# One pool for the feed-forward part, down's operand halves in freed slots, and early sum chains in a seven-product SwiGLU

## The chip, the core and the metric

The kernel runs on one core of a Trainium2 chip. The metric is the device time of one execution in microseconds (us). TensorE (PE in the profile) multiplies; ScalarE (ACT) and VectorE (DVE) convert, add and copy; GpSimd (POOL) and SyncE (SP) here mostly start DMAs. A DMA that adds to what is in the tile (an accumulating DMA) is started by POOL, a plain load by SP. Each engine works through a list of instructions whose order was fixed when the kernel was built; an instruction that waits holds up all behind it on its engine.

## The reference, cut to what matters

Two layers: a dilated-window attention layer and a gated-linear-attention layer (GLA), each followed by a feed-forward part. With 512 tokens, width 1024 and hidden width 2816, that part is

```python
def swiglu(h, w_gate_up, w_down):
    g, u = jnp.split(h @ w_gate_up, 2, axis=-1)
    return (jax.nn.silu(g) * u) @ w_down
# h += swiglu(rms_norm(h, ffn_norm[i]), ffn_w_gate_up[i], ffn_w_down[i])
```

It is run twice: FFN0 after attention, FFN1 after GLA. All is float32. To reach that accuracy each operand is split into a high part (rounded to the type fp32r) and a low part (what is left), and each product is three matmuls: high·high, high·low, low·high.

## The kernel before, in words

**A split** (`split`, lines 88 to 94) is one ACT instruction that writes the high tile (L92) and one DVE instruction that writes the low tile (L93). Weights arrive by DMA in a raw tile (`wf`, two buffers, or `wA`, `wB`) and are split into `wh` and `wl` (three buffers each).

**Order.** The Tile framework fixes each engine's order at build time. It takes instructions as they become ready in its own model, the ones with the smaller program number first; `high_priority(offset=AHEAD)` lowers the numbers by 100. A tile has a tag, and a tag a number of buffers; a new tile waits until one of its tag's buffers has been released by all its users. Pools are opened and closed per stage; a tile in a new pool waits for the tiles of the closed pool whose memory it overlaps (`reuse_waits="tile"`).

**Gate and up by seven products.** `gate_up` (L302) runs over six chunks, j = 0 to 5, of hidden columns: five of 512, the last of 256. Each chunk has gate and up columns, and tokens and input features are halved, so that a chunk is a 2x2 by 2x2 block product; it is computed with seven products instead of eight. The weight blocks 0 to 3 are combined as they are loaded. For each chunk `forms` (L221) is a generator that yields the weights of the seven products in the order in which they are used:

| product | left side | weights | where the raw weights come from |
|---|---|---|---|
| first | A11 | block 0 | `wA`, loaded by SP |
| second | A12 | block 1 | `wf`, loaded by SP |
| fifth | S1 | 0+2 | block 2 added onto `wA` by a POOL DMA, after the first product's split has read `wA` |
| sixth | S2 | 0+2+3 | DVE adds block 3 (`wB`) to `wA` |
| third | S4 | 3 | `wB`; block 1 is then added onto `wA` by a POOL DMA |
| seventh | S3 | 3+2 | block 2 added onto `wB` by a POOL DMA, after the third product's split has read `wB` |
| fourth | A22 | 0+2+3+1 | `wA` |

A chunk of 512 has two tiles of each (n = 2), the last chunk one (n = 1). The last chunk already loads blocks 0 and 3 twice, so that it need not wait for a split before it adds; all of these loads and adds stand in `first()`. `wA` has four buffers and `wB` two, so that a later chunk's loads start when an earlier chunk's buffers come free. A product of a 512-wide chunk is 24 matmuls (`product`, L287). S1 to S4 are sums of the normed input's blocks, made by `block_sums` (L184) on ACT and DVE and split into `sh` and `sl`; the splits of A11 to A22 are made while the stage before writes its last results. While a chunk is multiplied, the four results of the chunk before are transposed on PE and copied by ACT (`turn`, L319): 22 tiles `acts`, the first 8 in tag `h`, the other 14 in tag `a`.

**Pools.** `swiglu` (L212) opens an outer pool with the `a` tiles, in it a pool `GATE_UP` (`sh`, `sl`, `wA`, `wB`, `g`, `Rc`), closes that and opens a pool `DOWN` with 40 half-size tiles `ah`.

**Down.** The 22 `acts` are split and multiplied with down's weights, eight output blocks m of 22 x 3 matmuls. The splits of acts 0 and 1 go to free `xs` tiles during the last chunk, and their six matmuls run before the last eight transposes; the splits of acts 2 to 21 follow in `down` (L408), in `ah` tiles.

Of the kernel before, what the change touches and what calls it, by code (L numbers as in the profile page):

```python
# [12 lines left out]
F32 = mybir.dt.float32  # L13
# [7 lines left out]
P = 128  # L21
# [16 lines left out]
class Trunk:  # L38
    def __init__(self, ctx, tc, ins):
# [10 lines left out]
    ATTN = {"qk": 20, "v": 8, "zs": 4, "wa": 4, "wb": 2, "sm": 3, "pt": 2, "ob": 2, "on": 2, "ao": 4,  # L50
            "tab": 2, "masks": 1, "ms": 1, "Rc": 1, "ebias": 1, "mst": 1,
            "qv": 2, "qr": 2, "qtmp": 2, "st": 2, "t2": 2, "stn": 2, "st0": 2, "mw": 2, "mL": 5}
    FFN = {"a": NH - KT}
    GATE_UP = {"sh": 4, "sl": 4, "wA": 4, "wB": 2, "g": 7, "Rc": 8}
    DOWN = {"ah": 2 * NH - 4}
    GLA = {"qk": 8, "r": 8, "v": 8, "wg": 1, "z": 1, "rs": 2, "A": 2, "qs": 6, "kT": 6, "e": 4, "y": 1, "c": 1, "wa": 3,
           "state": 6, "later": 1, "reset": 1, "Rc": 1, "mid": 2, "full": 4}
    PBUFS = {"pp": 4, "s": 2, "t": 1, "o": 1}
# [153 lines left out]
    def swiglu(self, layer, col_next):  # L212
        with self.phase(f"ffn{layer}", self.FFN):
            acts = []
            outer = self.local
            with self.phase(f"gate_up{layer}", self.GATE_UP):
                self.gate_up(layer, acts, outer)
            with self.phase(f"down{layer}", self.DOWN):
                self.down(layer, acts, col_next)

    def forms(self, dram, ahead=0):  # L221
        nc = self.nc
        n = dram.shape[1]
        raw = {}

        def load(block, tag):
            raw[tag] = []
            for i in range(n):
                w = self.t(tag, (P, 1024))
                nc.sync.dma_start(w, dram[block, i])  # L230
                raw[tag].append(w)

        def add(tag, block):
            for i in range(n):
                nc.gpsimd.dma_start(raw[tag][i], dram[block, i], accum_op=ALU.add)

        def ready(tag):
            return [self.split(w, (P, 1024), "wh", "wl") for w in raw[tag]]

        def first():  # L240
            load(0, "wA")
            if n == 1:
                whole = raw["wA"]
                load(0, "wA")
                add("wA", 2)
                load(3, "wB")
                raw["wC"] = raw["wB"]
                load(3, "wB")
                add("wB", 2)
                return [self.split(w, (P, 1024), "wh", "wl") for w in whole]  # L250
            return ready("wA")

        def second():
            load(1, "wf")
            return ready("wf")

        def fifth():
            if n > 1:
                add("wA", 2)
                load(3, "wB")  # L260
                raw["wC"] = raw["wB"]
            return ready("wA")

        def sixth():
            for i in range(n):
                nc.vector.tensor_add(raw["wA"][i], raw["wA"][i], raw["wC"][i])
            return ready("wA")

        def third():
            add("wA", 1)  # L270
            return ready("wC")

        def seventh():
            if n > 1:
                add("wB", 2)
            return ready("wB")

        def fourth():
            return ready("wA")

        for step in (first, second, fifth, sixth, third, seventh, fourth):
            with self.tc.high_priority(offset=AHEAD + ahead):
                w = step()
            ahead = 0
            yield w
# [13 lines left out]
                mm(a, lhsT=xh[:, tok], rhs=wl[:, f], start=False, stop=False, skip_group_check=True)  # L299
                mm(a, lhsT=xl[:, tok], rhs=wh[:, f], start=False, stop=k == last, skip_group_check=True)  # L300

    def gate_up(self, layer, acts, outer):  # L302
        nc = self.nc
        self.col0 = 16 + 8 * layer
        ACT, DVE = nc.scalar.activation, nc.vector
        weights = [self.forms(self.ins["gate_up"][layer, j], 0 if j else 2 * AHEAD) for j in range(5)]
        weights.append(self.forms(self.ins["gate_up_last"][layer]))
        first = next(weights[0])
        self.minus = self.t("Rc", (P, 8))
        DVE.tensor_scalar(self.minus[:, 0:4], self.cols[:, self.col0 + 4:self.col0 + 8], -1.0, None, op0=ALU.mult)  # L310
        sums = [self.block_sums(m) for m in range(KT // 2)]
        self.kept = self.dr.tile([KT, P, S], F32, name=f"h_dram_{layer}")
        cut = lambda lo: [tuple(e[:, lo:lo + 256] for e in self.x[m]) for m in range(KT // 2, KT)]
        A11, A12, A22 = self.x[0:KT // 2], cut(0), cut(256)
        S3, S1, S2, S4 = ([s[i] for s in sums] for i in range(4))

        done = None

        def turn(c):  # L319
            if done is None:  # L320
                return
            pt = self.p("to"[c % 2])
            for i in range(NT):
                nc.tensor.transpose(pt[:, i * P:(i + 1) * P], done[i // 2][:, i % 2, c * P:(c + 1) * P], self.ident)
            if len(acts) < KT:
                a = self.t("h")
            else:
                self.n += 1
                a = outer.tile([P, S], F32, tag="a", name=f"a_{self.n}", bufs=NH - KT)
            ACT(a, pt, AF.Copy)  # L330
            acts.append(a)

        for j in range(6):
            width = 512 if j < 5 else 256
            w = weights[j]
            pair = lambda tag: [self.p(tag) for _ in range(2)]
            keep = lambda: self.t("g", (P, 2, S))

            def copy(src):
                out = keep()  # L340
                for i in range(2):
                    ACT(out[:, i, 0:width], src[i][:, 0:width], AF.Copy)
                return out

            b1 = pair("pp")
            self.product(b1, A11, first if j == 0 else next(w), width, True)
            turn(0)
            g1 = copy(b1)
            b2 = pair("pp")
            self.product(b2, A12, next(w), width, True)  # L350
            turn(1)
            if j == 0:
                for m in range(KT):
                    self.add_square(m, self.h[m], ("sq", "R")[m % 2])
                R = self.token_norm()
                for m in range(KT):
                    nc.gpsimd.dma_start(self.kept[m], self.h[m])
            for i in range(2):
                e = g1[:, i, 0:width]
                DVE.tensor_add(e, b2[i][:, 0:width], e)  # L360
                silu = ACT(e, e, AF.Silu, scale=R[:, i:i + 1])
            b3 = pair("s")
            self.product(b3, S1, next(w), width, True)
            turn(2)
            p5 = copy(b3)
            self.product(b1, S2, next(w), width, False)
            turn(3)
            h1 = copy(b1)
            self.product(b3, S4, next(w), width, False)
            for i in range(2):  # L370
                e = h1[:, i, 0:width]
                DVE.tensor_add(e, b3[i][:, 0:width], e)
                DVE.scalar_tensor_tensor(e, e, R[:, 4 + i:5 + i], g1[:, i, 0:width], op0=ALU.mult, op1=ALU.mult)
            self.product(b1, S3, next(w), width, False)
            h2 = copy(b1)
            for i in range(2):
                e = h2[:, i, 0:width]
                DVE.tensor_add(e, p5[:, i, 0:width], e)
            self.product(b1, A22, next(w), width, False)
            g2 = keep()  # L380
            for i in range(2):
                e = g2[:, i, 0:width]
                silu = ACT(e, b1[i][:, 0:width], AF.Silu, scale=R[:, 2 + i:3 + i])
                u = h2[:, i, 0:width]
                DVE.scalar_tensor_tensor(u, u, R[:, 6 + i:7 + i], e, op0=ALU.mult, op1=ALU.mult)
            done = (h1, h2)
            if j == 4:
                with self.tc.high_priority(offset=AHEAD):
                    early = [self.split(a, (P, S), "xs", "xs") for a in acts[0:2]]
        self.started = self.down_part(self.p("pp"), layer, 0, 0, 2, early)  # L390
        for c in range(2):
            turn(c)
        with self.tc.issue_after(silu.ins):
            nc.scalar.preload_act_table_set("natural_log_exp_and_others")

    def down_part(self, ps, layer, m, k, end, pairs):
        for k0, kn in ((0, 8), (8, 8), (16, 6)):
# [10 lines left out]
    def down(self, layer, acts, col_next):  # L408
        nc = self.nc
        ps, pairs = self.started  # L410
        for k in range(2, NH):
            if k < 8:
                with self.tc.high_priority(offset=AHEAD):
                    pairs.append(self.split(acts[k], (P, S), "ah", "ah"))
            else:
                pairs.append(self.split(acts[k], (P, S), "ah", "ah"))
        self.x = [None] * KT
        for m in range(KT):
            if m > 0:
# [656 lines left out]
```

## Time and profile before

| what | value |
|---|---|
| median of 3 runs | 1584.66 us (1582.45 to 1586.26) |
| the profiled execution | 1582.96 us |
| its span, first to last instruction | 1581.2 us |
| ACT, busy share of the span | 49% |
| DVE, busy share of the span | 60% |
| mean TensorE clock granted | 0.992 |
| moved by DMA | 179.74 MB |

The profile describes one execution. PE is nearly always busy, so what matters are the few places where it waits: a row such as `[3.71 <-ACT wh L92]` says that PE sat idle for 3.71 us before the instruction and that ACT's write of a `wh` tile in line 92 ended the wait. The granted clock (PEclk) is a share of full speed.

FFN0 multiplies from about 632 us of the span, its down part from 864 us; FFN1 from about 1224 us, its down part from 1454 us.

### The profile page before, as it was taken

The numbers are of one execution on the slowest core, as the hardware profiler recorded it, in microseconds if no ns is written. First come the engines' busy times: TensorE is split into PE (matmuls) and PEld (weight loads), VectorE is DVE, ScalarE is ACT, GpSimd is POOL, SyncE is SP. The second block draws the span as 40 slices with busy tenths as digits, with TensorE's granted clock in tenths as the row PEclk, the third lists the DMA queues.
The fourth block names the chain that finished last, engine by engine and source line by source line (L and its number), as shares of the span: only waits on it lengthen the run. The fifth ranks groups of instructions, "written<-read, shape, count | busy, mean of one in ns | idle before, by whom it ended". The sixth has DMA issues, their size and how long they took to land.

```text
span 1581.2 us, 21054 instructions
## 1 busy us (share of the span) xinstructions
PE 1550.1 (98%) x8078; PEld 1257.4 (80%) x8078; DVE 949.4 (60%) x1714; ACT 780.0 (49%) x1319; POOL 104.1 (7%) x180
## 2 busy tenths in 40 slices
PE   8999999999999999999999999999999999999999
PEld 7878787887877877788888888777778788878887
DVE  6574656666467656866666533756566766657421
ACT  6343443445345554665556422544564665556311
POOL 0001010101000001111110000000001111110000
PEclk9999999999999999999999999999999999999999
DMA  8422222242221215567674432311126567664331
GB/s 281 137 68 93 70 81 80 68 132 81 88 65 50 71 36 194 132 148 173 160 160 104 117 102 78 108 67 67 60 74 212 147 160 169 155 145 107 120 119 65
DMA packets 58964, 179.74 MB, mean 114 GB/s; under 512 B 9936, under 2 KB 10512, under 8 KB 58864
## 3 DMA queue, kind: packets, MB, share of 16 engines
q1 hardware_dynamic: 45776, 135.27, 26.1%
q0 software_dynamic: 13088, 43.13, 14.3%
q8 instruction: 63, 1.03, 0.3%
q14 instruction: 37, 0.30, 0.1%
HBM read 169.91 MB, written 8.46 MB: 113 GB/s over the span
## 4 chain that ended last, share of the span: by engine, by line
PE 75%; issue 13%; DVE 5%; ACT 3%; DMA 2%; POOL 2%; POOLq 0%; SPq 0%; ACTq 0%; DVEq 0%
PE ppp L511 8%; PE ppp L509 8%; PE ppp L510 8%; PE ppp L105 8%; PE ppp L104 8%; PE ppp L106 8%; PE po L618 4%; PE ppp L298 3%; PE ppp L299 3%; PE ppp L300 3%; DMA wB<-in_gate_up_dram 2%; PE ps L686 2%; PE pt L556 1%; PE ps L636 1%; PE po L938 1%
## 5 line engine op out<-in xcount | busy, mean ns | idle before, releaser
L93 DVE TENSOR_TENSOR wl<-wf,wh 128x1024 fp32r<-128x1024 f32 (+1 forms) x180 | 213.5, 1186 | 208.6 <-ACT wh L92 207.6
L92 ACT ACTIVATE wh<-wf 128x1024 fp32r<-128x1024 f32 (+1 forms) x180 | 185.5, 1031 | 303.4 <-PE ppp L105 179.1
L509 PE MATMUL ppp<-wh,xs 128*128 128x512 f32 (+1 forms) x672 | 263.4, 394 | 5.4 <-ACT wh L92 5.4
L511 PE MATMUL ppp<-wh,xs 128*128 128x512 f32 (+1 forms) x672 | 263.1, 392 | 0.0
L510 PE MATMUL ppp<-wl,xs 128*128 128x512 f32 (+1 forms) x672 | 262.6, 391 | 0.0
L509 PEld LDWEIGHTS ppp<-wh,xs 128*128 128x128 f32 x672 | 128.2, 191 | 30.6 <-ACT wh L92 5.4
L511 PEld LDWEIGHTS ppp<-wh,xs 128*128 128x128 f32 x672 | 128.1, 191 | 23.4
L510 PEld LDWEIGHTS ppp<-wl,xs 128*128 128x128 f32 x672 | 128.4, 191 | 22.5 <-DVE wl L93 1.2
L93 DVE TENSOR_TENSOR wl<-wA,wh 128x1024 fp32r<-128x1024 f32 x88 | 107.2, 1221 | 48.3 <-ACT wh L92 48.3
L104 PE MATMUL ppp<-ah,wh 128*128 128x512 f32 x320 | 125.6, 392 | 2.2 <-ACT ah L92 2.2
L105 PE MATMUL ppp<-ah,wh 128*128 128x512 f32 x320 | 125.7, 393 | 0.5 <-DVE ah L93 0.5
L106 PE MATMUL ppp<-ah,wl 128*128 128x512 f32 x320 | 125.0, 391 | 0.0
L92 ACT ACTIVATE wh<-wA 128x1024 fp32r<-128x1024 f32 x88 | 92.5, 1056 | 51.1 <-PE ppp L300 37.6
L298 PE MATMUL ppp<-wh,xs 128*128 128x512 f32 (+1 forms) x288 | 108.4, 384 | 4.6 <-ACT wh L92 3.7
L299 PE MATMUL ppp<-wl,xs 128*128 128x512 f32 (+1 forms) x288 | 107.9, 375 | 1.3 <-DVE wl L93 1.3
L300 PE MATMUL ppp<-wh,xs 128*128 128x512 f32 (+1 forms) x288 | 107.7, 374 | 0.0
L93 DVE TENSOR_TENSOR wl<-wB,wh 128x1024 fp32r<-128x1024 f32 x44 | 53.9, 1224 | 86.7 <-ACT wh L92 86.7
L105 PE MATMUL ppp<-xs,wh 128*128 128x512 f32 x256 | 103.7, 405 | 1.1 <-DVE xs L93 1.1
L104 PE MATMUL ppp<-xs,wh 128*128 128x512 f32 x256 | 103.4, 405 | 0.0
L106 PE MATMUL ppp<-xs,wl 128*128 128x512 f32 x256 | 102.9, 402 | 0.0
L583 ACT ACTIVATE sm<-sm,st 128x160 f32<-128x160 f32 (+2 forms) x128 | 56.9, 446 | 43.0 <-DVE st L582 41.5
L299 PE MATMUL ppp<-wl,sh 128*128 128x512 f32 (+1 forms) x192 | 73.0, 380 | 4.7 <-DVE wl L93 4.7
(281 smaller groups left out, 2933.2 us busy)
## 6 DMA issues: line engine op xcount, KB each, us to landing
wA<-in_gate_up_dram POOLq DMA_DIRECT2D x40, 512.0 KB, 5.4
wf<-in_down_dram SPq DMA_DIRECT2D x32, 512.0 KB, 3.6
wf<-in_a_w_v_dram SPq DMA_DIRECT2D x20, 512.0 KB, 3.6
wf<-in_gate_up_dram SPq DMA_DIRECT2D x20, 512.0 KB, 5.0
wA<-in_gate_up_dram SPq DMA_DIRECT2D x20, 512.0 KB, 4.3
wB<-in_gate_up_dram SPq DMA_DIRECT2D x20, 512.0 KB, 3.3
wB<-in_gate_up_dram POOLq DMA_DIRECT2D x20, 512.0 KB, 5.8
wf<-in_a_w_q_dram SPq DMA_DIRECT2D x16, 512.0 KB, 3.2
```

Source lines behind the costliest of these rows:

```text
L92: nc.scalar.activation(hi, src, AF.Copy)
L93: nc.vector.tensor_sub(lo, src, hi.bitcast(F32))
L104: mm(out, lhsT=wh, rhs=xh, start=start, stop=False)
L105: mm(out, lhsT=wh, rhs=xl, start=False, stop=False)
L106: mm(out, lhsT=wl, rhs=xh, start=False, stop=stop)
L298: mm(a, lhsT=xh[:, tok], rhs=wh[:, f], start=start and k == 0, stop=False, skip_group_check=True)
L299: mm(a, lhsT=xh[:, tok], rhs=wl[:, f], start=False, stop=False, skip_group_check=True)
L300: mm(a, lhsT=xl[:, tok], rhs=wh[:, f], start=False, stop=k == last, skip_group_check=True)
L509: mm(a, lhsT=xh, rhs=wh[:, f], start=k == 0, stop=False)
L510: mm(a, lhsT=xh, rhs=wl[:, f], start=False, stop=False)
L511: mm(a, lhsT=xl, rhs=wh[:, f], start=False, stop=k == KT - 1)
L618: self.nc.tensor.matmul(o, lhsT=pts[b][c], rhs=vals(i0 + b, c), start=c == 0, stop=c == 1)
```

## The change

1. `swiglu` opens one pool for gate, up and down together. The pool `DOWN` and its `ah` tiles go away.
2. `halves(a, k)` replaces the splits of acts 2 to 21: the high and the low part stand in one (128, 1024) tile, in a buffer of the tags that gate and up have finished with: `wA` for k = 2 to 5, `wB` for 6 and 7, `sh` for 8 to 11, `sl` for 12 to 15, `g` for 16 to 21.
3. The halves of acts 2 to 7 are traced at the end of `gate_up`, ahead of down's first six matmuls and of the last transposes, with high priority. Before, they were traced in `down`.
4. In chunk 0 and in the last chunk (`own`), `first()` loads block 0 into `wf`. Their sums get raw tiles of their own, which no split reads first: `sums()` loads block 0 into `wA` and adds block 2, loads block 3 into `wB` and once more into a second `wA` buffer, and adds block 2 onto that. `sums()` stands at the head of `second()`, ahead of the load of block 1. Chunk 0 so loads blocks 0 and 3 twice, as the last chunk did before: four more loads of 512 KB in each feed-forward part. Chunks 1 to 4 are as before.

```diff
-    FFN = {"a": NH - KT}
-    GATE_UP = {"sh": 4, "sl": 4, "wA": 4, "wB": 2, "g": 7, "Rc": 8}
-    DOWN = {"ah": 2 * NH - 4}
+    FFN = {"a": NH - KT, "sh": 4, "sl": 4, "wA": 4, "wB": 2, "g": 7, "Rc": 8}
...
         with self.phase(f"ffn{layer}", self.FFN):
             acts = []
-            outer = self.local
-            with self.phase(f"gate_up{layer}", self.GATE_UP):
-                self.gate_up(layer, acts, outer)
-            with self.phase(f"down{layer}", self.DOWN):
-                self.down(layer, acts, col_next)
+            self.gate_up(layer, acts)
+            self.down(layer, acts, col_next)
...
+        def sums():
+            load(0, "wA")
+            add("wA", 2)
+            load(3, "wB")
+            raw["wC"] = raw["wB"]
+            load(3, "wB", "wA")
+            add("wB", 2)
+
         def first():
-            load(0, "wA")
-            if n == 1:
-                whole = raw["wA"]
+            if not own:
                 load(0, "wA")
-                add("wA", 2)
-                load(3, "wB")
-                raw["wC"] = raw["wB"]
-                load(3, "wB")
-                add("wB", 2)
-                return [self.split(w, (P, 1024), "wh", "wl") for w in whole]
-            return ready("wA")
+                return ready("wA")
+            load(0, "wf")
+            return ready("wf")
 
         def second():
+            if own:
+                sums()
             load(1, "wf")
             return ready("wf")
...
-        weights = [self.forms(self.ins["gate_up"][layer, j], 0 if j else 2 * AHEAD) for j in range(5)]
-        weights.append(self.forms(self.ins["gate_up_last"][layer]))
+        weights = [self.forms(self.ins["gate_up"][layer, j], j == 0, 0 if j else 2 * AHEAD) for j in range(5)]
+        weights.append(self.forms(self.ins["gate_up_last"][layer], True))
...
+        with self.tc.high_priority(offset=AHEAD):
+            early += [self.halves(acts[k], k) for k in range(2, 8)]
         self.started = self.down_part(self.p("pp"), layer, 0, 0, 2, early)
...
+    def halves(self, a, k):
+        nc = self.nc
+        tag = "g" if k > 15 else "sl" if k > 11 else "sh" if k > 7 else "wB" if k > 5 else "wA"
+        both = self.t(tag, (P, 1024), F32R)
+        hi, lo = both[:, 0:S], both[:, S:]
+        nc.scalar.activation(hi, a, AF.Copy)
+        nc.vector.tensor_sub(lo, a, hi.bitcast(F32))
+        return hi, lo
...
-        for k in range(2, NH):
-            if k < 8:
-                with self.tc.high_priority(offset=AHEAD):
-                    pairs.append(self.split(acts[k], (P, S), "ah", "ah"))
-            else:
-                pairs.append(self.split(acts[k], (P, S), "ah", "ah"))
+        for k in range(len(pairs), NH):
+            pairs.append(self.halves(acts[k], k))
```

In the parts that the diff cuts, `fifth()` and `seventh()` test `own` where they tested n, and a tile of `turn` is taken from the one pool.

More of the change, by code (lines that the diff above doesn't have):

```diff
@@ L214, in swiglu, with forms @@
             acts = []
-            outer = self.local
-            with self.phase(f"gate_up{layer}", self.GATE_UP):
-                self.gate_up(layer, acts, outer)
-            with self.phase(f"down{layer}", self.DOWN):
-                self.down(layer, acts, col_next)
-    def forms(self, dram, ahead=0):
+            self.gate_up(layer, acts)
+            self.down(layer, acts, col_next)
+    def forms(self, dram, own, ahead=0):
         nc = self.nc
@@ L224, in forms, with load @@
         raw = {}
-        def load(block, tag):
+        def load(block, tag, at=None):
             raw[tag] = []
             for i in range(n):
-                w = self.t(tag, (P, 1024))
+                w = self.t(at or tag, (P, 1024))
                 nc.sync.dma_start(w, dram[block, i])
@@ L257, in fifth @@
         def fifth():
-            if n > 1:
+            if not own:
                 add("wA", 2)
@@ L273, in seventh @@
         def seventh():
-            if n > 1:
+            if not own:
                 add("wB", 2)
@@ L300, in product, with gate_up @@
                 mm(a, lhsT=xl[:, tok], rhs=wh[:, f], start=False, stop=k == last, skip_group_check=True)
-    def gate_up(self, layer, acts, outer):
+    def gate_up(self, layer, acts):
         nc = self.nc
@@ L324, in turn @@
                 nc.tensor.transpose(pt[:, i * P:(i + 1) * P], done[i // 2][:, i % 2, c * P:(c + 1) * P], self.ident)
-            if len(acts) < KT:
-                a = self.t("h")
-            else:
-                self.n += 1
-                a = outer.tile([P, S], F32, tag="a", name=f"a_{self.n}", bufs=NH - KT)
+            a = self.t("h" if len(acts) < KT else "a")
             ACT(a, pt, AF.Copy)
@@ L410, in down @@
         ps, pairs = self.started
-        for k in range(2, NH):
-            if k < 8:
-                with self.tc.high_priority(offset=AHEAD):
-                    pairs.append(self.split(acts[k], (P, S), "ah", "ah"))
-            else:
-                pairs.append(self.split(acts[k], (P, S), "ah", "ah"))
+        for k in range(len(pairs), NH):
+            pairs.append(self.halves(acts[k], k))
         self.x = [None] * KT
```

## The prediction

> **What bounds the kernel now.** I read the page first, then the waits of PE by stage, then the stretches around them.
>
> ```profile
> PE 1550.1 (98%) x8078; PEld 1257.4 (80%) x8078; DVE 949.4 (60%) x1714; ACT 780.0 (49%) x1319; POOL 104.1 (7%) x180
> ```
>
> ```profile
> 799.41 0.39 PE L300 MATMUL ppp<-wh,xs 128*128 128x512 f32 x1
> ...
> 804.85 0.40 PE L300 MATMUL ppp<-wh,xs 128*128 128x512 f32 x1
> ```
>
> PE is the bound. In steady state 24 matmuls take 804.85 - 799.41 = 5.44 us: 0.227 each, 5.44 a product. The change removes no matmul, so it can win only what PE loses around the feed-forward parts. The rows of PE's waits there, as total, times and longest:
>
> FFN0, start (627 to 638 us):
>
> ```profile
> PE ppp L298 <- ACT wh L92: 3.7, 1, 3.7
> PE ppp L299 <- DVE wl L93: 1.3, 1, 1.3
> ```
>
> FFN0, end of chunk 0 (663 to 674):
>
> ```profile
> PE ppp L299 <- DVE wl L93: 1.5, 2, 0.8
> PE ppp L298 <- ACT g L342: 0.9, 1, 0.9
> PE ppp L298 <- ACT wh L92: 0.2, 1, 0.2
> ```
>
> FFN1, end of chunk 0 (1251 to 1260):
>
> ```profile
> PE ppp L299 <- DVE wl L93: 1.0, 2, 0.8
> PE ppp L298 <- ACT wh L92: 0.3, 1, 0.3
> ```
>
> Chunk 4 in FFN0 (827 to 834), then in FFN1 (1397 to 1420):
>
> ```profile
> PE ppp L299 <- DVE wl L93: 1.2, 2, 0.7
> ```
>
> ```profile
> PE ppp L299 <- DVE wl L93: 1.0, 2, 0.8
> PE ppp L298 <- ACT wh L92: 0.8, 1, 0.8
> ```
>
> Start of down, FFN0 and FFN1, from PE's timeline:
>
> ```profile
> 866.61 0.33 PE L324 MATMUL pt<-ident,g 128*128 128x128 f32 x1 [0.52 <-DVE g L385]
> 866.77 0.27 PE L324 MATMUL po<-ident,g 128*128 128x128 f32 x1
> 868.14 0.50 PE L104 MATMUL ppp<-ah,wh 128*128 128x512 f32 x1 [1.10 <-ACT ah L92]
> 868.87 0.50 PE L105 MATMUL ppp<-ah,wh 128*128 128x512 f32 x1 [0.23 <-DVE ah L93]
> ```
>
> ```profile
> 1456.21 0.27 PE L324 MATMUL po<-ident,g 128*128 128x128 f32 x1
> 1457.57 0.50 PE L104 MATMUL ppp<-ah,wh 128*128 128x512 f32 x1 [1.09 <-ACT ah L92]
> ```
>
> Start to start a wait costs more than its idle figure: 868.87 - 868.14 = 0.73 where 0.227 is usual is 0.50 lost for an idle 0.23. I add 0.25 a wait.
>
> The stretches (length, busy us by engine, granted clock, DMA share, GB/s):
>
> ```profile
> core 0: us, PE busy (x) PEld busy (x) DVE busy (x) ACT busy (x) POOL busy (x), PEclk, DMA share, GB/s
> 617.50:629.60 12.10, 10.88 (x48) 8.66 (x47) 10.45 (x18) 7.78 (x14) 4.02 (x8) 1.00 1.01 383
> 629.60:659.50 29.90, 26.11 (x106) 20.92 (x106) 29.29 (x42) 21.13 (x27) 5.53 (x7) 0.89 0.58 138
> 632.00:636.00 4.00, 2.61 (x5) 1.66 (x6) 4.00 (x7) 3.60 (x5) 0.90 (x1) 0.50 0.00 1
> 841.50:864.20 22.70, 22.70 (x187) 22.18 (x186) 14.29 (x19) 14.15 (x24) 0.86 (x1) 1.00 0.29 66
> 868.00:872.00 4.00, 3.63 (x9) 2.41 (x10) 3.57 (x6) 4.00 (x9) 0.00 (x0) 0.70 0.69 209
> 1455.00:1460.00 5.00, 3.10 (x14) 1.73 (x13) 3.12 (x6) 4.86 (x9) 0.00 (x0) 1.00 0.55 171
> ```
>
> Two things stand here beside the waits. After the waits at FFN0's start and at its down the clock was granted at 0.50 and 0.70. And from 629.6 to 659.5 DVE is busy for 29.29 of 29.90 us: behind PE's wait stands a second limit.
>
> **The change part by part** (plus is time won).
>
> *Start of FFN0.* A split of weights, low part and high part:
>
> ```profile
> L93 DVE TENSOR_TENSOR wl<-wf,wh 128x1024 fp32r<-128x1024 f32 (+1 forms) x180 | 213.5, 1186 | 208.6 <-ACT wh L92 207.6
> L92 ACT ACTIVATE wh<-wf 128x1024 fp32r<-128x1024 f32 (+1 forms) x180 | 185.5, 1031 | 303.4 <-PE ppp L105 179.1
> ```
>
> 1.03 + 1.19 = 2.2 one after the other. Lost now: 3.7 + 1.3 + 2 x 0.25 = 5.5, and half of the 2.61 us that PE was busy at clock 0.50, 1.3: together 6.8. Block 0 now takes SP's first places:
>
> ```profile
> 611.50 4.41 SPq L230 DMA_DIRECT2D wf<-in_gate_up_dram  x2
> 615.96 0.92 SPq L230 DMA_DIRECT2D wA<-in_gate_up_dram  x2
> 617.53 0.81 SPq L230 DMA_DIRECT2D wB<-in_gate_up_dram  x2
> 618.38 0.92 SPq L230 DMA_DIRECT2D wA<-in_gate_up_dram  x2
> ```
>
> So far the two `wf` loads from 611.50 on were block 1, for the second product. With block 0 there, its splits are done before the stage ahead ends (632.09 less the wait, about 628.4), and the first product starts at once. But block 1 now has to wait until those splits release `wf`, and six loads of the sums (615.96 to 619.3) are ahead of it on SP's queue. They are 3.1 MB; the eight copies of h are 2 MB, the four additions another 2 MB: 7.1 MB at the 383 GB/s of the row are 18.5 us from 616, so 634.5; block 1's own 1 MB makes 637.2, and ACT's and DVE's 2.2 us of split bring 639.4. PE asks for it at 628.4 + 5.44 = 633.8. That is a new wait of 5.6 us, and again a slow clock, 1.3: 6.9 lost for 6.8 won. ACT and DVE may run other sums first, which moves it further; so -0.5. Bounds: +6.8 if block 1 comes in time (DVE's rows leave 1.65 + 0.61 us of its own idle time, so 2.3 is likelier even then), and -7 if ACT and DVE take it up only halfway through DVE's full stretch, at 645.
>
> *Seventh product of chunk 0.* Its weights no longer wait for third's splits: they are a tile of their own, whose addition is set off at the start. The three rows of FFN0 and the two of FFN1 go: 2.6 + 4 x 0.25 = 3.6 and 1.3 + 3 x 0.25 = 2.0. What is late next is only the copy of b1 between seventh and fourth, already in the 0.9. Bounds of the sum: 0 to 5.6. In FFN1 the stage before has long products, SP's queue is ahead, and I expect no wait for block 1. All four `wA` buffers are now in use in chunk 0, so chunk 1's first load moves from 618 to seventh's splits. Two products, 10.9 us, hide it:
>
> ```profile
> wA<-in_gate_up_dram SPq DMA_DIRECT2D x20, 512.0 KB, 4.3
> ```
>
> 4.3 and a split of 2.2. Without that cover it costs the excess one for one.
>
> *Start of down.* Acts 2 to 7 are split before the last transposes. In FFN0 1.37 - 0.1 and 0.50 come back, and of the slow stretch 3.63 x 0.30 = 1.1: 2.9. In FFN1 1.36 - 0.1 and, taken as in FFN0, 0.5: 1.8. Together 4.7. The wait of 0.52 stays; if PE takes the new matmuls first, two times 0.5 more. Bounds 0 (see the rivals) to 5.7. Acts 8 on are split behind it; at about 0.7 each on DVE against 0.68 of PE each, with six acts in hand, they keep ahead.
>
> By a rule of the Trainium skill, "TensorE: Matmul & The Clock Gate", section "Why this matters for your kernels", the clock falls after PE gaps of more than about 3 us. By it these 1.1 would not come back, and the sum below would be 1.1 less. The trace speaks against a simple reading on one side (clock 0.70 where no wait is over 1.10) and for it on the other (1.00 in FFN1 after the same gap).
>
> *Last chunk.* Six high and six low parts are added to it. From the first rows of that kind:
>
> ```profile
> L92 ACT ACTIVATE ah<-h x6: 621/628/631, 867.5 to 870.5; 128x512 fp32r<-128x512 f32 x6
> L93 DVE TENSOR_TENSOR ah<-h,ah x6: 681/684/694, 868.1 to 871.5; 128x512 fp32r<-128x512 f32 x6
> ```
>
> 6 x 0.628 = 3.8 on ACT, 6 x 0.684 = 4.1 on DVE, in a stretch of 22.70 us where they are busy 14.15 and 14.29: it fits, but each may hold up a split. -0.5 for both parts; bounds 0 and -4.1.
>
> *Chunk 4.* POOL's queue, FFN1, and the landing times of the last two:
>
> ```profile
> 1386.40 0.86 POOL L235 DMA_DIRECT2D wA<-in_gate_up_last_dram  x1 [1.79 <-DMA wA<-in_gate_up_last_dram]
> 1386.93 1.21 POOL L235 DMA_DIRECT2D wA<-in_gate_up_dram  x1
> ```
>
> ```profile
> wA<-in_gate_up_last_dram POOLq DMA_DIRECT2D x1, 512.0 KB, 7.6
> wA<-in_gate_up_dram POOLq DMA_DIRECT2D x1, 512.0 KB, 11.8
> ```
>
> An addition for the last chunk stands ahead of chunk 4's own, which then takes 11.8 us instead of 7.6: 4.2 more. That makes chunk 4's sums late. The change moves the last chunk's sums from `first()` to `second()`, but what they wait for is a free `wA` buffer, and that comes at the same time, a chunk ahead. Both additions can now go there, since the second has a `wA` buffer too, not a `wB` one. So one more addition ahead of chunk 4's: up to 4.2 more in each part. FFN0 has some slack, its row being 1.2. I take -3 for both; bounds +3.0 (all rows of chunk 4 gone) and -8.4.
>
> *The one pool* I put at 0 (+1 to -1): its halves live until down's last block, as `ah` did, and GLA begins with projections that need base tiles alone.
>
> Sum: -0.5 + 5.6 + 4.7 - 0.5 - 3 = 6.3 us won. From the profiled execution's 1582.96 (span 1581.2 and 1.8 around it) that makes 1576.7; from the median, 1.7 higher, 1578.4. I predict 1577.
>
> **The rivals.**
>
> *More than that.* Block 1 lands in time and the additions do not hurt chunk 4: 2.3 + 5.6 + 4.7 = 12.6, so 1570; with PE's whole 6.8 at the start 17, so 1566. For it: the loads of 615.96 on have waited for nothing. Against: the load of SP's queue and DVE's full stretch.
>
> *No change.* Chunk 4 pays in full, -8.4 instead of -3: 0.9 won, 1582. For it stands the 11.8; against, that the first of the two additions can be through before chunk 4's first. Here belongs also that the change does not do what it says: if acts 2 to 7 get their buffers only after the last chunk's own splits, or their order stays, the 4.7 stay away, and 1.6 is won: 1581. Two `wA` buffers, of chunk 4, are free well before.
>
> *Slower.* At FFN0's start ACT and DVE, whose order is fixed, have all sums of S1 to S4 ahead of block 1's split. With the other terms, 5.6 + 4.7 - 0.5 - 3 = 6.8, and a wait of x for block 1, the sum is 6.8 - x - 1.3 + 6.8 = 12.3 - x. It is below -3.2 from x = 15.5 on: a split of block 1 that ends after 649.3. At 652 it is 5.9 slower: 1589. For it: DVE is full until 659.5, so its sums could fill this time. Against: high priority, and a landing at 637.
>
> **How the numbers follow.** 0.2%, 3.2 us, is about what a measurement of this kernel can tell from no change. Against 1584.66 faster means below 1581.5. The forecast has 0.50 (its own range 1572 to 1581), more than that 0.18, no change 0.18, slower 0.14. Faster is the first two, 0.68; same 0.18; slower 0.14. Leaving out a tenth at each end gives 1567 to 1588.
>
> **What would show it.** Right: no wait of 3.7 before FFN0's first product, but one before the second for `wh` or `wl`, with a landing of `wf` near 637; no wait for L93 at the end of chunk 0; down's first halves in ACT's and DVE's rows ahead of the last transposes, and only the 0.52 there; two additions for the last chunk among chunk 4's first ones, and chunk 4's rows longer. It is wrong if block 1's wait is over 12 us or absent, if the transposes are still followed by 1.1 us of waiting, if chunk 4's rows vanish, or if PE waits anywhere outside the feed-forward parts where it did not.

## The result and the profile after

The changed kernel takes 1589.73 us (median of 13 runs, 1583.12 to 1593.74), the kernel before 1584.0 beside it (13 runs, 1579.93 to 1590.49). The ratio is 1.0033, 95% interval 1.0016 to 1.0049: slower by about 5 us. The prediction was 1577 (1567 to 1588), faster.

The first thing to notice is that the two profiled executions do not show this. Their spans are equal, 1581.2 us before and 1581.0 after, but the profiled execution of after is the fastest of its 13, at a granted clock of 0.995 (before: 0.992); the median clock of those 13 is 0.990. Span times clock is 1568.6 before and 1573.1 after, so at one clock the changed kernel has lost some 4 to 5 us. Part of the difference lies where the change has no instruction. The rows of the stretches up to FFN0's first product (columns as in the prediction: stretch, length, then PE busy) for before, after, and a run of the experiments below:

```profile
0.00:632.09 632.09, 621.45 (x3713) 500.85 (x3713) 397.51 (x1025) 298.72 (x660) 42.76 (x106) 0.99 0.31 100
```

```profile
0.00:626.60 626.60, 619.26 (x3713) 499.50 (x3713) 394.24 (x1016) 295.50 (x656) 41.80 (x105) 1.00 0.31 96
```

```profile
0.00:633.54 633.54, 626.24 (x3713) 504.60 (x3713) 394.68 (x1016) 295.45 (x656) 41.80 (x105) 0.98 0.29 95
```

The third row is the run `after_addheld`, whose work up to there is that of after. The same 3713 matmuls keep PE busy for 619.26 us in one and 626.24 in the other, with the granted clock 1.00 and 0.98. Against before's 621.45 after's profile has 2.2 us less of PE time there for the same matmuls, so I read gains and losses stage by stage, not from the span. A chunk's length is counted from the start of its first matmul to that of the next chunk's. "Down" goes from its first matmul behind the last product to the start of its last in FFN0, and to the end of the span in FFN1, which is some 3.7 us behind the last matmul there.

| stage | before | after | predicted gain | gain |
|---|---|---|---|---|
| FFN0, where chunk 1 starts | 679.00 | 679.04 | +3.1 (start -0.5, seventh +3.6) | 0; -2.2 without the clock's share |
| FFN1, chunk 0 | 41.80 | 40.71 | +2.0 | +1.1 |
| chunk 4, FFN0 and FFN1 | 42.03, 44.87 | 48.01, 48.30 | -3 | -9.4 |
| last chunk, FFN0 and FFN1 | 22.45, 22.45 | 22.65, 22.63 | -0.5 | -0.4 |
| down, FFN0 and FFN1 | 125.21, 127.64 | 120.17, 124.10 | +4.7 | +8.6 |

**FFN0's start.** PE's timeline of after has the first product without any wait, and no wait before the second. The fifth waits instead:

```profile
626.60 0.39 PE L297 MATMUL ppp<-wh,xs 128*128 128x512 f32 x1
...
637.25 0.39 PE L299 MATMUL ppp<-wh,xs 128*128 128x512 f32 x1
642.31 0.73 PE L297 MATMUL ps<-wh,sh 128*128 128x512 f32 x2 [4.67 <-ACT sh L90]
646.24 0.80 PE L298 MATMUL ps<-wl,sh 128*128 128x512 f32 x1 [3.19 <-DVE wl L91]
```

The row of ACT behind it, and the queues of POOL and SP:

```profile
640.26 1.06 ACT L90 ACTIVATE wh<-wA 128x1024 fp32r<-128x1024 f32 x1 [8.46 <-DMA wA<-in_gate_up_dram]
641.22 1.99 ACT L90 ACTIVATE sh<-g 128x1024 fp32r<-128x1024 f32 x2
```

```profile
629.92 0.91 POOL L230 DMA_DIRECT2D wA<-in_gate_up_dram  x1 [1.60 <-PE ppp L299]
```

```profile
609.88 14.29 SPq L225 DMA_DIRECT2D wf<-in_gate_up_dram  x4
624.22 0.92 SPq L225 DMA_DIRECT2D wA<-in_gate_up_dram  x2
```

Read from the last fence upwards. On SP's queue four `wf` loads stand first: block 0 and block 1. `wf` has two buffers, so block 1's loads wait there until block 0 has been split, and the sums' loads behind them start at 624.22 where the prediction had them at 615.96. The addition of block 2 starts at 629.92 and its data is there at 640.26, where ACT has sat for 8.46 us, with the splits `sh<-g` of the fifth product's other side behind it in its order. What the first product gains, the fifth gives back and more: chunk 1 starts at the same time, although PE's work ahead of FFN0 took 2.2 us less.

**Chunk 4.** PE's waits there, FFN0 (813 to 842) and the two longest of FFN1 (1400 to 1430):

```profile
PE ppp L297 <- ACT g L337: 1.4, 1, 1.4
PE ppp L298 <- DVE wl L91: 0.9, 2, 0.8
PE ps L298 <- DVE wl L91: 0.8, 1, 0.8
PE ppp L297 <- ACT wh L90: 0.7, 1, 0.7
PE ps L297 <- ACT wh L90: 0.7, 1, 0.7
```

```profile
PE ppp L297 <- ACT g L337: 2.2, 1, 2.2
PE ps L297 <- ACT wh L90: 1.5, 1, 1.5
```

POOL's queue in FFN0, and the times from issue to landing of its first and last entry:

```profile
797.89 0.88 POOL L230 DMA_DIRECT2D wA<-in_gate_up_last_dram  x1 [14.63 <-DVE g L373]
798.43 1.24 POOL L230 DMA_DIRECT2D wA<-in_gate_up_dram  x1
799.50 1.06 POOL L230 DMA_DIRECT2D wA<-in_gate_up_last_dram  x1
800.04 1.41 POOL L230 DMA_DIRECT2D wA<-in_gate_up_dram  x1
```

```profile
wA<-in_gate_up_last_dram POOLq DMA_DIRECT2D x1, 512.0 KB, 5.5
...
wA<-in_gate_up_dram POOLq DMA_DIRECT2D x1, 512.0 KB, 13.5
```

Two additions for the last chunk stand among chunk 4's own, as predicted, and chunk 4's second one takes 13.5 us (9.5 in the kernel before, where one addition for the last chunk stands ahead of it). But the rows for `ACT g L337`, the longest, have nothing to do with weights: that is the copy of a product out of PSUM, the memory that PE writes to. They are the part that was not foreseen.

**Down.** The transposes are followed by the halves' matmuls at once, and the 0.52 before the transposes is gone too:

```profile
870.99 0.49 PE L323 MATMUL pt<-ident,g 128*128 128x128 f32 x3
871.32 0.49 PE L323 MATMUL po<-ident,g 128*128 128x128 f32 x3
871.56 0.47 PE L102 MATMUL ppp<-wA,wh 128*128 128x512 f32 x1
```

### The profile page after: what moved, and what is told of

Read it like the earlier page. It is cut to its first block, busy times and chain, and to the rows that moved or that the text cites. A ratio compares the mean times of both kernels' runs of the same rounds, so it can differ in the third digit from the quotient of the medians.

```text
span 1581.0 us, 21074 instructions
## 1 busy us (share of the span) xinstructions
PE 1545.3 (98%) x8078; PEld 1256.1 (79%) x8078; DVE 948.3 (60%) x1714; ACT 778.0 (49%) x1319; POOL 104.1 (7%) x180
## 3 DMA queue, kind: packets, MB, share of 16 engines
HBM read 174.11 MB, written 8.46 MB: 115 GB/s over the span
## 4 chain that ended last, share of the span: by engine, by line
PE 81%; DVE 8%; DMA 5%; ACT 3%; issue 2%; POOL 0%; SPq 0%; POOLq 0%; ACTq 0%; DVEq 0%
PE ppp L513 8%; PE ppp L511 8%; PE ppp L102 8%; PE ppp L103 8%; PE ppp L512 8%; PE ppp L104 8%; PE ppp L297 5%; PE ppp L299 4%; PE ppp L298 4%; PE po L620 4%; DMA wA<-in_gate_up_dram 2%; DVE wl L91 2%; PE ps L297 2%; PE ps L299 2%; PE ps L298 2%
## 5 line engine op out<-in xcount | busy, mean ns | idle before, releaser
L91 DVE TENSOR_TENSOR wl<-wf,wh 128x1024 fp32r<-128x1024 f32 (+1 forms) x186 | 220.8, 1187 | 216.0 <-ACT wh L90 215.1
L90 ACT ACTIVATE wh<-wf 128x1024 fp32r<-128x1024 f32 (+1 forms) x186 | 191.8, 1031 | 308.7 <-PE ppp L103 177.7
L511 PEld LDWEIGHTS ppp<-wh,xs 128*128 128x128 f32 x672 | 127.6, 190 | 30.4 <-ACT wh L90 5.7
L513 PEld LDWEIGHTS ppp<-wh,xs 128*128 128x128 f32 x672 | 127.6, 190 | 23.2 <-issue 0.2
L91 DVE TENSOR_TENSOR wl<-wB,wh 128x1024 fp32r<-128x1024 f32 x38 | 46.5, 1225 | 72.7 <-ACT wh L90 72.7
L297 PE MATMUL ps<-wh,sh 128*128 128x512 f32 (+1 forms) x192 | 74.4, 388 | 7.1 <-ACT sh L90 4.9
L298 PE MATMUL ps<-wl,sh 128*128 128x512 f32 (+1 forms) x192 | 73.3, 382 | 4.7 <-DVE wl L91 4.7
L297 PE MATMUL ppp<-wh,sh 128*128 128x512 f32 (+1 forms) x192 | 73.0, 381 | 0.8 <-ACT wh L90 0.7
```

The source lines that it names most:

```text
L90: nc.scalar.activation(hi, src, AF.Copy)
L91: nc.vector.tensor_sub(lo, src, hi.bitcast(F32))
L297: mm(a, lhsT=xh[:, tok], rhs=wh[:, f], start=start and k == 0, stop=False, skip_group_check=True)
L511: mm(a, lhsT=xh, rhs=wh[:, f], start=k == 0, stop=False)
L513: mm(a, lhsT=xl, rhs=wh[:, f], start=False, stop=k == KT - 1)
```

## The experiments

All were timed in five rounds beside the kernel before, in four sessions (a_halves to d_last, a_held to both_held, before_addheld to both_noadd0, both_sums_first). The kernel before had medians of 1583.73, 1584.6, 1582.03 and 1584.74 in them, so kernels of different sessions are compared by their ratios. Chunk and down lengths are from the profiles, in the manner of the table above; "chunk 1" is the time at which FFN0's chunk 1 starts.

| run | median us | ratio to before (95%) | chunk 4, FFN0 / FFN1 | chunk 1 | down, FFN0 / FFN1 |
|---|---|---|---|---|---|
| before | 1584.0 | 1 | 42.0 / 44.9 | 679.0 | 125.2 / 127.6 |
| after | 1589.73 | 1.0033 (1.0016-1.0049) | 48.0 / 48.3 | 679.0 | 120.2 / 124.1 |
| a_halves | 1584.3 | 0.9991 (0.9975-1.0007) | 44.6 / 48.4 | 684.0 | 120.2 / 124.1 |
| b_sums | 1593.13 | 1.0065 (1.0047-1.0083) | 46.5 / 47.8 | 678.9 | 125.4 / 129.0 |
| c_chunk0 | 1581.73 | 0.9988 (0.9971-1.0005) | 44.9 / 48.1 | 681.6 | 120.2 / 124.2 |
| d_last | 1591.55 | 1.0047 (1.0030-1.0064) | 48.6 / 47.3 | 680.3 | 120.2 / 124.1 |
| a_held | 1575.6 | 0.9944 (0.9926-0.9961) | 42.2 / 44.6 | 679.9 | 120.2 / 124.1 |
| after_held | 1585.98 | 1.0006 (0.9988-1.0025) | 45.7 / 46.1 | 680.8 | 120.2 / 124.1 |
| after_addheld | 1576.65 | 0.9940 (0.9921-0.9960) | 41.8 / 42.1 | 686.4 | 120.2 / 124.1 |
| both_held | 1571.56 | 0.9915 (0.9899-0.9930) | 40.2 / 40.3 | 680.9 | 120.2 / 124.1 |
| before_addheld | 1579.33 | 0.9981 (0.9966-0.9996) | 40.2 / 40.2 | 678.6 | 125.4 / 129.2 |
| both_ffn1 | 1569.61 | 0.9914 (0.9892-0.9937) | 40.2 / 40.2 | 679.2 | 120.2 / 124.3 |
| both_c0old | 1569.63 | 0.9920 (0.9898-0.9942) | 40.2 / 40.2 | 681.7 | 120.2 / 124.1 |
| both_noadd0 | 1565.29 | 0.9893 (0.9869-0.9918) | 40.2 / 40.2 | 676.1 | 120.2 / 124.1 |
| both_sums_first | 1569.85 | 0.9913 (0.9893-0.9933) | 40.3 / 40.2 | 680.4 | 120.2 / 124.1 |

### First four: which part costs

My theory was that the loss lies in the sum chains alone (part 4 of the change): chunk 4's additions behind the last chunk's, and chunk 0's fifth product. The rivals were a cost of the one pool and the halves (parts 1 to 3), and that only the granted clock moves the median.

**a_halves**: parts 1 to 3 without part 4.

```diff
-        weights = [self.forms(self.ins["gate_up"][layer, j], j == 0, 0 if j else 2 * AHEAD) for j in range(5)]
-        weights.append(self.forms(self.ins["gate_up_last"][layer], True))
+        weights = [self.forms(self.ins["gate_up"][layer, j], False, 0 if j else 2 * AHEAD) for j in range(5)]
+        weights.append(self.forms(self.ins["gate_up_last"][layer], "old"))
```

("old" stands for the last chunk's loads as before, all in `first()`.)

> One pool and down's halves as in the changed kernel, the sum chains as before (the last chunk reads block 0 into wA twice again, chunk 0's S1 waits for its plain load and sums later). If the loss sits in the sum chains (chunk 0's fifth product waiting for its addition, the last chunk's additions queued ahead of chunk 4's): both down stages keep their gain (5.0 and 3.5 us) and chunk 4 takes its 42 and 45 us again, so about 1575 to 1578, 0.5% faster than the kernel before. If the one pool and the halves on ScalarE and VectorE cost in the last chunk: no faster than before, 1584 or more, with chunk 4 or 5 still long. If the stage times are not what moves the median and only the granted clock is: within 0.15% of before.

**b_sums**: the kernel before, its pools and its down, with `own` and `sums()` of the changed kernel.

> The pools and down's halves of the kernel before, the sum chains set off on their own as in the changed kernel. If the loss sits in the sum chains: chunk 4 takes 48 us in both layers (before 42 and 45), chunk 0 of the first layer 3 to 6 us longer than before's 46.9, down as before, so 1590 to 1595, 0.4 to 0.7% slower than before, slower than the changed kernel too. If the pools and halves cost: about 1584 or less.

**c_chunk0** and **d_last**: the changed kernel with own sums in chunk 0 only (second line as in a_halves), and in the last chunk only (first line as in a_halves).

> The changed kernel with the last chunk's sums as before; chunk 0's on their own. If the sum chains are the loss: chunk 4 back to 42 and 45 us, so 9 us less than the changed kernel, 1578 to 1582; the first layer's chunk 0 still waits for its fifth product (52 us, of which 5.5 us may come back ahead of its first product). If chunk 4's length comes from the halves or the one pool: chunk 4 stays at 48 us and the time at 1586 to 1590.

> The changed kernel with chunk 0's sums as before; the last chunk's on their own. If the sum chains are the loss: chunk 4 at 48 us in both layers, the start of the first feed-forward stage as before (waits before its first product, 47 us for chunk 0), so 1583 to 1588: the down gain of 8.5 against chunk 4's 9.4. If chunk 4's additions aren't the cause, chunk 4 is at 42 and 45 us and the time at 1576.

b_sums and d_last are slower, as the theory says (d_last, at 1591.55, by more than the 1583 to 1588 expected). But a_halves did not win its 8.5 us of down: its chunk 4 takes 44.6 and 48.4 us with the additions in the order of before, and c_chunk0 the same. So "the sum chains alone" falls; in FFN1 either part alone lengthens chunk 4 by 3 to 3.5 us. Against the clock alone speaks that c_chunk0 and d_last, which differ only in which of the two chunks has its sums early, are 0.6% apart, 9.8 us. But their profiled executions are only 2.1 us apart (1582.28 and 1584.34, the latter the fastest of its 12), so where the rest of the 9.8 goes is not shown.

What a_halves shows, on ACT first, then in PE's waits of chunk 4:

```profile
841.44 0.63 ACT L411 ACTIVATE wA<-h 128x512 fp32r<-128x512 f32 x1 [3.34 <-DVE wl L91]
841.98 1.04 ACT L90 ACTIVATE wh<-wA 128x1024 fp32r<-128x1024 f32 x1
842.92 0.58 ACT L350 ACTIVATE g<-ppp 128x512 f32<-128x512 f32 x1
```

```profile
PE ppp L310 <- ACT g L350: 2.2, 1, 2.2
PE ppp L311 <- DVE wl L91: 1.3, 2, 0.8
```

The first of the halves (L411) stands in ACT's order in the middle of chunk 4. Its `wA` buffer comes free when DVE has split the weights in it, so ACT waits for 3.34 us, and the next splits and the copy of a finished product (L350) wait behind it. PE needs that copy's PSUM tile for the next product: 2.2 us. The new theory: chunk 4 has two causes, the halves' wait for a buffer at the head of ACT's order, and the additions on POOL's queue.

### Second four: hold one, hold the other, hold both

**a_held**: a_halves with the halves held until the last chunk's first copy is past; **after_held** is after with the same edit. `issue_after` keeps what is built under it behind a given instruction in the fixed order. `mark` is the last ACT instruction of `g1 = copy(b1)`, at the end of the loop that of the last chunk.

```diff
+            mark = copied[-1]
...
-        with self.tc.high_priority(offset=AHEAD):
+        with self.tc.issue_after(mark.ins), self.tc.high_priority(offset=AHEAD):
             early += [self.halves(acts[k], k) for k in range(2, 8)]
```

**after_addheld**: after with the last chunk's two additions held behind chunk 4's last; **both_held** has both edits. `self.added` is the addition traced last so far, and `after` is `issue_after`, or nothing where there is none.

```diff
+            own_chain = self.added
             load(0, "wA")
-            add("wA", 2)
+            with self.after(own_chain):
+                add("wA", 2)
...
-            add("wB", 2)
+            with self.after(own_chain):
+                add("wB", 2)
```

> One pool, halves, sums as before, and the six halves of tiles 2 to 7 held in ScalarE's and VectorE's order until the last chunk's first copy is past. If the halves' wait for a slot, ahead of chunk 4's copies, is what lengthens chunk 4: chunk 4 at 42 and 45 us (44.6 and 48.4 with the halves unheld), down still 120.2 and 124.1, so 6 us under the run without the hold, about 0.5% faster than before. If the one pool itself (or the early loads that it allows) lengthens chunk 4: 44.6 and 48.4 stay, and the time with them.

> The changed kernel with the six halves held as in a_held; the sum chains on their own. If chunk 4 has two causes, the halves and the additions that stand behind the last chunk's: only the halves' goes, chunk 4 at about 46.5 and 47.8 us as with the sum chains alone, so 1 to 3 us under the changed kernel, 0.1 to 0.2% slower than before. If the halves are the only cause: 42 and 45 us and 0.4% faster than before. If the additions are the only one: nothing changes.

> The changed kernel with the last chunk's first two additions held on GpSimd's queue until chunk 4's last addition has been issued; the halves unheld. If there are two causes: chunk 4 at about 44.6 and 48.4 us as with the halves alone, 3 to 4 us under the changed kernel, within 0.15% of before. If the additions are the only cause: 42 and 45 us, 0.4% faster than before.

> The changed kernel with both holds. With two causes and no third: chunk 4 at 42 and 45 us, down at 120.2 and 124.1, so 8 to 9 us under the changed kernel, 0.4 to 0.5% faster than before, as fast as a_held or up to 2 us faster (chunk 0's own sums). If something else in the one pool costs: chunk 4 stays over 44 and 47 us.

The table of chunk 4 (FFN0 / FFN1) for the four kernels with part 4, as length in us, the time in it that PE was idle, and the granted clock:

| | halves free | halves held |
|---|---|---|
| additions free | 48.0 / 48.3, idle 4.6 / 5.2, clock 0.96 / 0.96 | 45.7 / 46.1, idle 3.8 / 4.1, clock 1.00 / 1.00 |
| additions held | 41.8 / 42.1, idle 1.5 / 1.8, clock 1.00 / 1.00 | 40.2 / 40.3, idle 0 / 0, clock 1.00 / 1.00 |

Both causes are there, and no third: with both held PE does not wait in chunk 4 at all. The row of both_held in FFN0 shows PE busy for its whole length (FFN1: 40.27 of 40.27):

```profile
801.34:841.53 40.19, 40.19 (x186) 32.98 (x184) 25.49 (x27) 23.51 (x31) 6.08 (x7) 1.00 0.73 156
```

PE's waits keep the two apart. With only the additions held, the one wait left in FFN0's chunk 4 is that for a copy of a product:

```profile
PE ppp L304 <- ACT g L345: 1.5, 1, 1.5
```

With only the halves held, that wait is gone and those for `wh` and `wl` stay.

Three expectations missed. After_addheld was to be at 44.6 and 48.4, as a_halves; it is at 41.8 and 42.1. A_halves is no run of the halves alone: one addition for the last chunk stands ahead of chunk 4's there, as in before. After_held was to be at 46.5 and 47.8, as b_sums; it is at 45.7 and 46.1, with the clock at 1.00 where b_sums has 0.96. And both_held goes under before's own chunk 4 of 42.0 and 44.9: the kernel before was paying for the queue already. It beats both kernels, at 0.9915.

### Third four: before's own queue, and chunk 0

**before_addheld**: the kernel before with the two additions held in the same way. **both_ffn1**: both_held with `own` in chunk 0 for the second layer only (`j == 0 and layer == 1`). **both_c0old**: with no own sums in chunk 0. **both_noadd0**: both_held without the first layer's additions of block 2 in chunk 0, so that its sums lack that block.

> The kernel before, alone changed in that the last chunk's two additions are held on GpSimd's queue until chunk 4's last addition has been issued. If the queue order is a cost of its own, the kernel before pays part of it already (chunk 4 at 42.0 and 44.9 us against 40.2 for a chunk without waits): 40.2 in both layers, 6 us less, 0.35 to 0.4% faster than before. If those 1.8 and 4.7 us have another cause, or the last chunk now waits for its late additions: no change.

> The kernel with both holds, but with chunk 0's sums on their own in the second layer only. If the first layer's chunk 0 gives back at its fifth product what its early first product wins: within 2 us of both holds in full (0.9915), the first layer's first product at 632 us instead of 628 and chunk 1 from the same 680 us. If the early start is worth something: 3 to 5 us slower than that.

> The kernel with both holds and chunk 0's sums as before in both layers. The last chunk's sums alone are on their own. If chunk 0's own sums are worth what the second layer's rows say: 0.5 to 1 us slower than both_ffn1, 0.9915 to 0.993. If they cost in the first layer: 1 to 3 us faster than both holds in full.

> The kernel with both holds; left out are the four additions of block 2 in the first layer's chunk 0 (its sums lack that block, in that chunk and layer alone). If those additions are what the fifth product waits for: its two waits (4.6 and 2.8 us) go and chunk 0 takes 44 to 46 us instead of 52.4, 6 to 8 us under both holds in full, 0.9865 to 0.988. If ScalarE's and VectorE's splits of the sums S1 hold it by themselves: chunk 0 stays over 50 us.

Before_addheld has chunk 4 at 40.2 in both layers; its row of POOL's queue and the landing behind it:

```profile
798.03 0.88 POOL L235 DMA_DIRECT2D wA<-in_gate_up_dram  x1 [14.78 <-DVE g L381]
799.72 0.87 POOL L235 DMA_DIRECT2D wA<-in_gate_up_dram  x1 [0.81 <-DVE wl L93]
```

```profile
wA<-in_gate_up_dram POOLq DMA_DIRECT2D x1, 512.0 KB, 6.3
```

Chunk 4's second addition lands in 6.3 us where nothing of the last chunk is ahead of it (9.5 in before, 13.5 in after), and the last chunk is no longer for it (22.44 and 22.46 against 22.45). The chunks give the 6.4 us that were expected; the median gives 2.7 of them (0.9981, interval 0.9966 to 0.9996). Its profile's FFN1 down is 1.6 longer than before's, with the same three waits but a clock of 0.83 in its first 10 us, where before's profile has 1.00; the rest of the gap is not explained.

Both_ffn1, both_c0old and both_held lie within one interval: chunk 0's own sums are worth nothing that these runs can tell, in either layer. FFN1's chunk 0 takes 40.6 to 40.9 us in all three, 40.8 where its sums are as before, and 40.9 in before_addheld, so the gain of 1.1 in the first table does not belong to them either.

Both_noadd0 takes 45.9 us for FFN0's chunk 0 where both_held takes 52.4. Of these 6.5 us 4.5 are PE's idle time (9.4 and 5.0) and 2.0 its busy time, at a clock of 0.93 against 1.00. Of the fifth product's waits, 4.6 and 2.8 us in both_held, one of 1.2 stays, and one of 2.1 for `wh` follows it. The ratio of 0.9893 (interval 0.9869 to 0.9918) is 3.5 us under both_held's, short of the 6 to 8 expected.

### The last: the order that the prediction had assumed

**both_sums_first**: both_held with block 1's loads of chunk 0 held behind the sums' loads. `self.loaded` is the load built last so far.

```diff
+            hold = None
             if own:
                 sums()
-            load(1, "wf")
+                hold = self.loaded
+            with self.after(hold if n > 1 else None):
+                load(1, "wf")
```

> The kernel with both holds, and in chunk 0 the six loads of the sums issued on SyncE's queue ahead of block 1's two loads, the order that the prediction had assumed. If the fifth product of the first layer waits because the sums' loads stand behind block 1's, which wait for free buffers: the first addition of chunk 0 starts up to 6 us sooner and the two waits of the fifth product (4.6 and 2.8 us) shrink by as much. Then either block 1 is late in its turn, with a wait of some 5 us ahead of the second product as predicted (0.991 to 0.992 again), or it is not and the time falls by 3 to 6 us (0.9875 to 0.9895). If the sums' loads are early enough now and only the additions are slow: both waits stay and the time with them, 0.9915.

The sums' loads now start at 616.47, and the fifth product waits for nothing. PE's two waits from 620 to 680 stand in the second product:

```profile
616.47 0.90 SPq L229 DMA_DIRECT2D wA<-in_gate_up_dram  x2
...
620.17 6.13 SPq L229 DMA_DIRECT2D wf<-in_gate_up_dram  x2
```

```profile
PE ppp L307 <- ACT wh L91: 9.3, 1, 9.3
PE ppp L308 <- DVE wl L92: 0.4, 1, 0.4
```

```profile
641.57 1.06 ACT L91 ACTIVATE sh<-g 128x1024 fp32r<-128x1024 f32 x1 [0.90 <-DVE g L195]
642.53 1.99 ACT L91 ACTIVATE wh<-wf 128x1024 fp32r<-128x1024 f32 x2
```

The four additions start at 630.50, directly behind the last copy of h on POOL's queue and only 1.4 us sooner than in both_held (631.90; up to 6 were expected). What spares the fifth product its wait is that the second one now waits longer. This is the predicted wait at its predicted place, 9.3 us instead of 5.6. ACT's row 642.53 has no wait of its own: block 1's split stands in ACT's order behind splits of S1 to S4 that wait for DVE (three times up to here, 4.5 us in all). That is the mechanism of the rival "slower", at x = 9.7 instead of the 15.5 from which it would have decided. The time does not move (0.9913): chunk 1 starts at 680.4 against 680.9. In either order FFN0's chunk 0 is far over the 40.2 of an undisturbed chunk (51.6 and 52.4), because of the additions in one and of block 1's late split in the other.

## Why the prediction was wrong

**Chunk 4 is the step that failed.** Its mechanism was there (one more addition of the last chunk on POOL's queue), its size was not: -3, with a bound of -8.4, against -9.4. The rows of chunk 4 before and after, FFN0 first, then FFN1:

```profile
799.64:841.66 42.02, 40.80 (x185) 32.87 (x184) 25.48 (x27) 23.15 (x31) 6.06 (x7) 1.00 0.71 150
799.40:847.41 48.01, 43.44 (x185) 34.00 (x184) 27.30 (x30) 24.59 (x34) 5.48 (x7) 0.96 0.65 142
```

```profile
1386.23:1431.10 44.87, 43.00 (x186) 33.89 (x185) 25.50 (x27) 23.15 (x31) 6.04 (x7) 0.96 0.65 138
1386.00:1434.30 48.30, 43.08 (x185) 33.92 (x184) 27.30 (x30) 24.71 (x34) 5.14 (x6) 0.96 0.62 140
```

Length less PE's busy time is its idle time: 1.22 and 4.57 in FFN0, 1.87 and 5.22 in FFN1, so 3.35 us more waiting in each. "FFN0 has some slack" was wrong: it lost as much waiting as FFN1. What FFN0 lost beyond that is busy time, 2.6 us for the same matmuls: four waits more, at 0.25 each as counted in the prediction, and a granted clock of 0.96 where it was 1.00. FFN1 had 0.96 already before. The sum's term for chunk 4 had no place for the clock. Nor is it settled by the waits alone: a_held's chunk 4 in FFN1 has 2.6 us of idle time and 1.00, before's has 1.87 and 0.96.

Of the 9.4 us the additions alone make 4.9 (after_held against before: 3.7 and 1.2), of the 6.7 us of added waiting 4.8.

**The other part of it was booked elsewhere, at nearly nothing.** The step "last chunk, -0.5" counted six halves as engine time in a stretch with room. The last chunk did lose only 0.4. But the halves did not all run there; the first of them stood in ACT's order in chunk 4, waiting for a buffer, where the prediction had "Two `wA` buffers, of chunk 4, are free well before". ACT in after, with the copy that PE waits for behind the half:

```profile
839.71 0.63 ACT L398 ACTIVATE wA<-h 128x512 fp32r<-128x512 f32 x1 [1.41 <-DVE wl L91]
840.25 1.04 ACT L90 ACTIVATE wh<-wA 128x1024 fp32r<-128x1024 f32 x1
841.19 0.58 ACT L337 ACTIVATE g<-ppp 128x512 f32<-128x512 f32 x1
```

Between after and after_held lie 4.5 us (2.3 and 2.2), of which 1.9 are waiting; the rest is busy time, at 0.96 in after and 1.00 in after_held. What an instruction holds up was not priced; only its duration was.

**FFN0's start and the seventh product**: predicted +3.1 together, measured 0, and -2.2 without the clock's share in the work ahead: a miss of 5.3, next to the 6.4 of chunk 4. One of the prediction's own signs of being wrong stands here: block 1's wait is absent. The first product did start at once, and the waits for L93 at the chunk's end are gone; a wait of 1.5 us for DVE's `g` (L368) before the transposes stands there instead. The new wait came before the fifth product, since SP's order was the reverse of the one assumed; both_sums_first shows the assumed order with the wait where it was put. The +3.6 of the seventh product was no separate gain: chunk 0 is bound by when its data is ready, and a wait that is removed at its end is replaced by one further ahead.

**Down** brought 8.6 instead of 4.7. The prediction left the 0.52 before the transposes standing; it went as well (0.73 start to start, in both layers). And a wait cost more there, beside its idle time, than was counted. FFN1 shows that without the clock, which is 1.00 in its first 10 us before and after: 1.9 us of the gain of 3.5 are idle time and 1.65 busy time (122.00 and 120.35), 0.55 for each of the three waits that went, where 0.25 was added. In FFN0 busy time fell by 3.2, so about 1.5 came back by the clock, where 1.1 was counted. The first 10 us of down: before in FFN0 and in FFN1, b_sums (without early halves) in FFN1, both_held (with them) in FFN0:

```profile
864.12:874.12 10.00, 8.16 (x31) 5.76 (x30) 6.83 (x11) 7.92 (x14) 0.00 (x0) 0.83 0.77 222
1453.55:1463.55 10.00, 8.10 (x38) 5.87 (x37) 6.84 (x11) 8.91 (x16) 0.00 (x0) 1.00 0.68 214
```

```profile
1459.46:1469.46 10.00, 8.16 (x31) 5.76 (x30) 6.83 (x11) 7.93 (x14) 0.00 (x0) 0.83 0.74 216
```

```profile
864.17:874.17 10.00, 10.00 (x50) 8.22 (x49) 9.86 (x16) 8.40 (x14) 0.00 (x0) 1.00 0.41 113
```

FFN0's down takes 125.2 to 125.4 us in all three kernels without early halves and 120.2 in all twelve with them. In each of the three, both down parts begin with the same waits of 0.5, 1.1 and 0.2 us within 3 us. In five of these six parts the clock was at 0.83 over the first 10 us; in FFN1 of before it stayed at 1.00, and that part is 1.4 and 1.6 us shorter than in b_sums and before_addheld. Without the waits it stayed at 1.00. The Trainium skill, "TensorE: Matmul & The Clock Gate", section "Why this matters for your kernels", warns of gaps of more than about 3 us between bursts of matmuls. The measurement decides against that figure as a safe limit.

**The sum**: 0 + 1.1 - 9.4 - 0.4 + 8.6 is about 0 in the two profiles, and about -2.3 with -2.2 for FFN0's start. The medians differ by 5. The other 3 us or so are not explained; after's profile is that of its fastest execution. The rival "no change" had chunk 4 at its full -8.4 and gave 1582; the mechanism that the rival "slower" named shows only in both_sums_first.

## What to carry to other kernels

An instruction that is set off early must be priced at the place where the engine's order puts it, by what stands behind it there while it waits, not by its duration in the stage that it was written for. On a queue that serves several stages, the next stage's transfers belong behind the current stage's last one: a hold for each of these two turned a change that lost 0.33% into one that wins 0.85% (0.9915), and the second alone helps the kernel before a little (0.9981). And where a stage is bound by the arrival of its data, as FFN0's chunk 0 is here, removing the wait of one step only moves it to another.

## What was not expected of the hardware

The landing time of an addition of 512 KB ranges from 5.5 us as the first to 13.5 as the fourth on POOL's queue within 2.2 us of issue. And the clock granted to identical work varied between executions by as much as the effect that was sought: 619.26 to 626.24 us of PE time for the same 3713 matmuls up to FFN0. A single profiled span could not tell these kernels apart. The stage lengths told most of them, but not all: c_chunk0 and d_last are 9.8 us apart in the median and 2.1 in their profiles. And the same short waits slowed the clock in some places and not in others, so a stage's length in one profile can be off by about 1.5 us for that alone.
